# Layer 1's output and MLP products as one 512-column and one 256-column product per k tile, and two adaLN k tiles left to TensorE

## Chip, cores and metric

The kernel runs on one core of one Trainium2 chip. The metric is the device time of one execution in microseconds; it was 1927.91 us as the median of three runs of the kernel before (1926.07 to 1928.13).

## What is computed

A two-layer diffusion trunk over 256 context tokens and 256 latent tokens of width 1024. Only the latent stream of the second layer is returned, so layer 1 needs its output product and its MLP for the 256 latent tokens alone. Cut to what matters here:

```python
sh1, sc1, ga1, sh2, sc2, ga2 = split((c_silu @ mod_w + mod_b), 6)      # adaLN, once for c and once for c_ctx
h = rms_norm(x, norm1_g) * (1 + sc1) + sh1
m = g1 * (y_lru @ w_branch[0]) + g2 * (y_gla @ w_branch[1]) + g3 * (y_att @ w_branch[2])
x = x + ga1 * (m @ w_out)
x = x + ga2 * (square(relu(modulate(x, norm2_g, sh2, sc2) @ mlp_w1)) @ mlp_w2)
```

Products are made to nearly full float32 precision from a rounded high part and a low part of each operand: W·x is taken as Wh·xh + Wh·xl + Wl·xh.

## The kernel before, in words

Activations lie with the channel in the partitions (8 k tiles of 128) and the 512 tokens (context first, then latent) along the free dimension. Every weight is a 128x1024 tile, that is 8 k tiles by 128 output channels. `weight` (L191 to L202) loads it on the SP queue (L194), ScalarE rounds it to the high part `wh` (L200) and VectorE subtracts to get the low part `wl` (L201); three pairs of `wh`, `wl` are kept. `gemm` (L252 to L263) makes one PSUM tile from a weight: for each k tile three matmuls, Wh·xh, Wh·xl and Wl·xh, 512 columns wide in layer 0 and 256 wide where only one half of the tokens is wanted. All matmuls are recorded by the helper `mm` (L212). PSUM has four tiles for these products.

The order around the change in each layer: the branches' `merge` products, where layer 0 has three of branch 1 and eight of branch 2 after the letter "u" of `QORD` (L30, and the loop from L905 on); the output product `out` (8 weights; in layer 0 done first for the context half and then for the latent half, from L938 on); `norm_stats` and `norm_apply` for the second norm after each half (L369 and L399); then the MLP in chunks: `up` (L961 to L967) with 32 weights `w1`, `down` (L969) with 32 weights `w2`. In layer 0 the first five `up` products of the first chunk are also done half by half. In layer 1 all of these are 256 columns wide. `residual` (L930 to L934) adds a product times a per-channel factor into x: one VectorE instruction per 256 columns (L933). `up` takes relu on ScalarE out of PSUM (L965), squares on VectorE out of PSUM (L966) and splits the result (`split_to`, L282 on ScalarE and L283 on VectorE). In layer 1 the high and the low part of an activation lie side by side in one tile: `ytiles` (L472) gives two views of one tile `yp`, with the high part in one 256-column half and the low part in the other. The normed activation has two tiles, `hh` and `hl` (L397).

The adaLN vectors of layer 0 that are not needed at the start (units 2 to 5 of `mod_w`) come from the generator `mods` (L310 to L350), spawned at "u" (L916). It works in halves of 512 output channels, h1 to h8 here: h1 and h2 are unit 2, the gate `ga1`; h3 to h6 are units 3 and 4, the shift and scale of the second norm; h7 and h8 are unit 5. For one half it loads 8 k tiles of `mod_w` (128x512, L319, into the ten buffers `t2` of the helper `tmp`), and for both token kinds sums them times the conditioning scalar: k tile 0 on ScalarE (L339), the other seven on VectorE (L341), so 14 VectorE instructions for a half. Then `mod_cols` (L288) sums over partitions on TensorE with the constant `pick` (8 matmuls, which the trace shows as 16), copies (L296), transposes, and adds the bias (L308). The generator is paced by a model clock that counts matmul columns: each yield (3.0 after each k tile, 2.0 before `mod_cols`) puts its next step that much later among the products. `need` forces the steps that are still missing: L924 asks for unit 2 before the output product, L953 for units 3 and 4 before the second norm's `norm_apply`. The order on an engine is then set by the scheduler of the framework, by priorities and buffers; `norm_stats` and `norm_apply` of the second norm carry a raised priority (L948 and L954).

Of the kernel before, what the change touches and what calls it, by code (L numbers as in the profile page):

```python
# [15 lines left out]
F32 = mybir.dt.float32  # L16
F32R = mybir.dt.float32r
# [6 lines left out]
KT = 8  # L24
# [13 lines left out]
GZP, G0P = 2, 6  # L38
AHEAD = 800
L_SM, L_PT = 4.0, 1.5  # L40
M_A, M_K, M_S = 300, 3.0, 2.0
NDVE = (0, 2, 5)
NL = 2
O_LX, O_LY, O_GQ, O_GK, O_GV, O_GR, O_GZ = 0, 1024, 2048, 2560, 3072, 4096, 5120
# [60 lines left out]
def trunk_kernel(ctx: ExitStack, tc: tile.TileContext, out: bass.AP, d: dict):  # L105
# [17 lines left out]
    def tmp():  # L123
        return t2.tile([128, 512], F32, name="t2")
# [54 lines left out]
    def load_x():  # L179
        x = bigp.tile([128, KT, T], F32, name="big")  # L180
        for k in range(0, KT, 2):
            nc.sync.dma_start(x[:, k:k + 2, :], d["xt"][:, k:k + 2, :])
        return x
# [42 lines left out]
    def tick():  # L226
        while not busy[0] and tasks:
            t = min(tasks, key=lambda t: t[0])
            if t[0] > clock[0]:
                break  # L230
            step(t)

    def spawn(gen):
        tasks.append([clock[0], gen])
# [17 lines left out]
    def gemm(w, xh, xl, c0, c1=T):  # L252
# [9 lines left out]
            mm(ps[:, :n], wl[:, k, :], a, start=False, stop=k == KT - 1)  # L262
        return ps[:, :n]  # L263

    def gemm_tok(l, c, hh, hl, ts):


        ps = {t: ps_mm.tile([128, 512], F32, name="mm") for t in ts}
        for j in range(4):
            wh, wl = (a.rearrange("p (k m) -> p k m", k=2) for a in weight(l, "tok", c, j))  # L270
            for t in ts:
                s = slice(128 * t, 128 * t + 128)
                for i in range(2):
                    k = 2 * j + i
                    tick()
                    mm(ps[t], hh[:, k, s], wh[:, i, :], start=k == 0, stop=False)
                    mm(ps[t], hh[:, k, s], wl[:, i, :], start=False, stop=False)
                    mm(ps[t], hl[:, k, s], wh[:, i, :], start=False, stop=k == KT - 1)
        return ps
# [27 lines left out]
            bia = pc(l, "modb", o, q * m).rearrange("p (j i) -> p j i", j=q).unsqueeze(3).to_broadcast([128, q, m, 2])  # L307
            V.tensor_tensor(dst, src[:, q * h:q * h + q], bia, op=ALU.add)  # L308

    def mods(l, us, pace):  # L310

        halves = [(u, j) for u in us for j in range(2)]

        def load(u, j, k):
            with tc.high_priority(M_A):
                t = tmp()
                nc.sync.dma_start(t, d["mod_w"][l, u][:, k, 512 * j:512 * j + 512])  # L319
            return t  # L320

        def turn():
            if last:
                for _ in last[0]:
                    pass
                if last[2]:
                    done.add((l, last[1]))

        last = None
        for u, j in halves:  # L330
            bs = (0, 1) if l == 0 or u < 2 else (1,)
            acc = [tmp() for _ in bs]
            nx = load(u, j, 0)
            for k in range(KT):
                t, nx = nx, load(u, j, k + 1) if k + 1 < KT else None
                for a, b in zip(acc, bs):
                    c = cs[:, k, b:b + 1]
                    if k == 0:
                        S.activation(a, t, AF.Copy, scale=c)  # L339
                    else:  # L340
                        V.scalar_tensor_tensor(a, t, c, a, op0=ALU.mult, op1=ALU.add)  # L341
                yield pace
            yield M_S
            g = mod_cols(l, 128, lambda i, acc=acc, bs=bs: (pick[:, bs[i], :], lambda c: acc[i][:, c:c + 128]),
                         len(bs), (4 * u if j == 0 else 8 + 4 * u,) if u < 2 else (8 * u + 4 * j,))
            next(g)
            turn()
            last = g, u, j
        yield pace
        turn()  # L350
# [42 lines left out]
    def norm_mul(l, which):  # L393

        a = sm.tile([128, 8, 2], F32, name="amul")
        g = pc(l, "n1" if which == 1 else "n2").unsqueeze(2).to_broadcast([128, 8, 2])
        return (hp.tile([128, KT, T], F32R, name="hh"), hp.tile([128, KT, T], F32R, name="hl"), a, g)  # L397

    def norm_apply(l, which, x, c0, c1, st, hn, ks):  # L399
        n = c1 - c0  # L400
        sh0, sc0 = (0, 8) if which == 1 else (24, 32)
        hh, hl, a, g = hn
        k0, k1, s0, s1 = ks[0], ks[-1] + 1, c0 // 256, c1 // 256
        V.scalar_tensor_tensor(a[:, k0:k1, s0:s1], modT[l][:, sc0 + k0:sc0 + k1, s0:s1], 1.0, g[:, k0:k1, s0:s1],
                               op0=ALU.add, op1=ALU.mult)
        for k in ks:
            h = tmp()
            if k % 2:
                G.tensor_tensor(h[:, :n], x[:, k, c0:c1], st[1][:, :n], op=ALU.mult)
            else:  # L410
                V.tensor_tensor(h[:, :n], x[:, k, c0:c1], st[0][:, :n], op=ALU.mult)
            for s in range(s0, s1):
                c = slice(256 * s - c0, 256 * s - c0 + 256)
                sc, sh = a[:, k, s:s + 1], modT[l][:, sh0 + k, s:s + 1]
                if k in NDVE:
                    V.tensor_scalar(h[:, c], h[:, c], sc, sh, op0=ALU.mult, op1=ALU.add)
                else:
                    S.activation(h[:, c], h[:, c], AF.Identity, scale=sc, bias=sh)
            split_to(hh[:, k, c0:c1], hl[:, k, c0:c1], h[:, :n])
# [41 lines left out]
    for l in range(NL):  # L461
# [443 lines left out]
        for st_ in QORD[l]:  # L905
            if st_ == "q":
                qs[len(qs)] = gqa_q(len(qs))
            elif st_ in "01":
                for g in ((0, 1), (2, 3)):
                    spawn(attend(int(st_), g, *qs[int(st_)]))  # L910
            elif st_ == "f":
                finish()
            elif st_ == "m":
                merge(1, next(mi), y2h, y2l)
            elif st_ == "u" and l == 0:
                spawn(mods(0, range(2, 6), M_K))  # L916
        if l:
            finish()
        mh, ml = ytiles("yh")
# [6 lines left out]
        V.tensor_scalar(ga, modT[l][:, 16:24, :], 0.5, None, op0=ALU.mult)  # L926
        if l == 0:
            x = load_x()

        def residual(i, ps, s0, a, b):  # L930
            for s in range(a // 256, b // 256):
                c = slice(256 * s, 256 * s + 256)
                V.scalar_tensor_tensor(x[:, i, c], ps[:, 256 * s - a:256 * s - a + 256], s0[:, i, s:s + 1], x[:, i, c],  # L933
                                       op0=ALU.mult, op1=ALU.add)  # L934
# [5 lines left out]
            mq = [mod_load(l, 5, h, ("yh", "yl")[h]) for h in range(2)]  # L940
        for a, b in halves:
            for i in range(8):
                residual(i, gemm(weight(l, "out", i), mh, ml, a, b), ga, a, b)
            if hn is None:
                hn = norm_mul(l, 2)
            if last:
                mod_half(l, 5, 0, mq[0])
            with tc.high_priority(NHP):  # L948
                st = norm_stats(x, a, b)
            if last:  # L950
                mod_half(l, 5, 1, mq[1])
                done.add((l, 5))
            need(l, 3, 4)  # L953
            with tc.high_priority(NHP):  # L954
                norm_apply(l, 2, x, a, b, st, hn, range(8))
# [4 lines left out]

        def up(c, i, a, b):  # L961
            uh, ul = hid[c]
            ps = gemm(weight(l, "w1", 8 * c + i), hh, hl, a, b)
            r, r2 = gtmp()[:, :b - a], gtmp()[:, :b - a]
            S.activation(r, ps, AF.Relu)  # L965
            V.scalar_tensor_tensor(r2, ps, 0.0, r, op0=ALU.max, op1=ALU.mult)  # L966
            split_to(uh[:, i, a:b], ul[:, i, a:b], r2)  # L967

        def down(c, i, a, b):  # L969
            residual(i, gemm(weight(l, "w2", c, i), *hid[c], a, b), modT[l][:, 40:48, :], a, b)  # L970

        for c in range(5):
            if c < 4:
                hid[c] = ytiles(("yh", "yl")[c % 2])
                n = NSPL if c == 0 and not last else 0
                for a, b in halves:
                    for i in range(n):
                        up(c, i, a, b)
                for i in range(n, 8):
                    up(c, i, c0, T)  # L980
            if c == 0:
                need(l, 5)
            if c == 4 and not last:
                need(1, 0, 1)
                hn1 = norm_mul(l + 1, 1)
                for a, b in halves[::-1]:
                    for i in range(8):
                        down(3, i, a, b)
                    with tc.high_priority(NHP):
                        norm_apply(l + 1, 1, x, a, b, norm_stats(x, a, b), hn1, range(8))  # L990
            elif c > 0:
                for i in range(8):
                    down(c - 1, i, c0, T)
                    if c == 4:
                        nc.sync.dma_start(out[:, i, :], x[:, i, 256:])
            if l == 0 and c == 0:
                spawn(mods(1, range(5), 1.5 * M_K))
        x1 = x


# [101 lines left out]
```

## Time and profile before

| | |
|---|---|
| median of three runs | 1927.91 us |
| the profiled execution, its own time | 1926.13 us |
| its span, first to last instruction | 1924.3 us |
| TensorE matmul busy | 1819.8 us (95%), 10696 instructions |
| VectorE busy | 1273.0 us (66%), 2137 instructions |
| ScalarE busy | 926.4 us (48%) |
| granted TensorE clock, mean | 0.98 |

Times in the rows are microseconds from the start of the span, unless marked ns. PE is TensorE's matmul side, PEld its weight loads, DVE VectorE, ACT ScalarE, POOL GpSimd, SP the queue that issues DMAs. A matmul's row is longer than the distance to the next one, because matmuls are pipelined; rates are therefore read from the distance between starts. A granted clock of 1.00 is 2.4 GHz, 0.50 is 1.2 GHz. "x16" merges that many instructions into one line, and the bracket at a line's end is the idle time before it and what ended it.

### The profile page before, as it was taken

The page shows a single profiled execution, that of the slowest core. Times are in us where ns is not written, and L with a number is a line of the kernel's source. Part 1 is how long each engine was busy: PE and PEld are TensorE (multiplying, and loading weights), DVE is VectorE, ACT ScalarE, POOL GpSimd, SP SyncE. Part 2 cuts the span into 40 slices and gives each one's busy share as a digit, 9 for nine tenths or more (in the row PEclk, how much of TensorE's full clock was granted, in tenths as well). Part 3 has the DMA queues.
Part 4 walks back from the last instruction along what each step waited for, and adds up shares of the span by engine and source line. Part 5 has one row for each costly group of instructions (what it writes and reads, how often), then busy time and mean ns, then how long its engine had stood idle before and what let it go on. Part 6 is the DMA issues. An engine that isn't in the chain of part 4 may idle for free.

```text
span 1924.3 us, 27716 instructions
## 1 busy us (share of the span) xinstructions
PE 1819.8 (95%) x10696; PEld 1544.4 (80%) x10696; DVE 1273.0 (66%) x2137; ACT 926.4 (48%) x1586; POOL 58.0 (3%) x88
## 2 busy tenths in 40 slices
PE   5998999999999999779999999996999999999999
PEld 4765778887777888778888889764888878999999
DVE  5677764445566984889854448787765677566665
ACT  3778544343443333454332325877654554445442
POOL 1000000000000000010000000000000000000000
PEclk9999999999999999879999999998999999999999
DMA  9322223222221653847643236531433333664654
GB/s 313 99 74 69 68 71 97 76 90 77 66 66 45 224 170 124 271 130 235 209 133 99 93 94 191 159 124 62 129 120 114 123 115 98 240 182 148 186 180 150
DMA packets 91619, 255.66 MB, mean 133 GB/s; under 512 B 9184, under 2 KB 20576, under 8 KB 91488
## 3 DMA queue, kind: packets, MB, share of 16 engines
q1 hardware_dynamic: 91488, 253.90, 41.6%
q8 instruction: 84, 1.38, 0.3%
q14 instruction: 47, 0.39, 0.1%
HBM read 252.82 MB, written 1.05 MB: 132 GB/s over the span
## 4 chain that ended last, share of the span: by engine, by line
PE 58%; issue 30%; DVE 6%; ACT 4%; POOL 1%; DMA 1%; SPq 0%; POOLq 0%; DVEq 0%; ACTq 0%
PE mm L212 49%; PE mx L212 2%; PE mx L744 1%; PE mx L725 1%; DVE wl L201 1%; ACT wh L200 1%; DVE t L341 1%; PE mx L216 1%; PE mx L699 1%; PE mx L510 1%; DMA t<-mod_w 1%; DVE lru L530 0%; PE mx L701 0%; DVE lru L529 0%; ACT lru L614 0%
## 5 line engine op out<-in xcount | busy, mean ns | idle before, releaser
L201 DVE TENSOR_TENSOR wl<-wraw,wh 128x1024 fp32r<-128x1024 f32 x365 | 445.9, 1224 | 297.7 <-ACT wh L200 294.5
L200 ACT CAST wh<-wraw 128x1024 fp32r<-128x1024 f32 x363 | 380.1, 1049 | 539.5 <-PE mm L212 464.2
L212 PE MATMUL mm<-hh,wh 128*128 128x512 f32 (+1 forms) x1448 | 500.3, 346 | 12.7 <-DVE big L933 6.1
L212 PE MATMUL mm<-hl,wh 128*128 128x512 f32 (+1 forms) x1448 | 496.4, 343 | 0.0
L212 PE MATMUL mm<-hh,wl 128*128 128x512 f32 (+1 forms) x1448 | 495.6, 342 | 0.0
L212 PEld LDWEIGHTS mm<-hh,wh 128*128 128x128 f32 x1448 | 276.3, 191 | 46.4 <-issue 9.6
L212 PEld LDWEIGHTS mm<-hl,wh 128*128 128x128 f32 x1448 | 276.0, 191 | 32.6 <-issue 3.5
L212 PEld LDWEIGHTS mm<-hh,wl 128*128 128x128 f32 x1448 | 275.8, 191 | 31.7 <-issue 1.4
L212 PE MATMUL mm<-yh,wh 128*128 128x512 f32 (+1 forms) x640 | 225.2, 352 | 3.3 <-DVE big L933 3.3
L212 PE MATMUL mm<-yh,wl 128*128 128x512 f32 (+1 forms) x640 | 225.0, 352 | 0.0
L212 PE MATMUL mm<-yl,wh 128*128 128x512 f32 (+1 forms) x640 | 223.3, 349 | 0.0
L212 PE MATMUL mm<-yp,wh 128*128 128x256 f32 x1024 | 190.6, 287 | 3.8 <-ACT g L771 2.3
L212 PEld LDWEIGHTS mm<-yp,wh 128*128 128x128 f32 x1024 | 161.1, 193 | 6.0 <-ACT g L771 2.5
L341 DVE SCALAR_TENSOR_TENSOR t<-t,cs,t 128x512 f32<-128x512 f32 x210 | 149.3, 752 | 12.7 <-DMA t<-mod_w 9.0
L212 PE MATMUL mm<-yp,wl 128*128 128x256 f32 x512 | 146.4, 286 | 0.8 <-DVE wl L201 0.8
L212 PEld LDWEIGHTS mm<-yh,wh 128*128 128x128 f32 x640 | 122.4, 191 | 18.7 <-DVE big L933 3.6
L212 PEld LDWEIGHTS mm<-yh,wl 128*128 128x128 f32 x640 | 122.1, 191 | 15.2 <-issue 0.5
L212 PEld LDWEIGHTS mm<-yl,wh 128*128 128x128 f32 x640 | 122.1, 191 | 14.9 <-issue 0.5
L212 PE MATMUL mm<-wh,hh 128*128 128x512 f32 x288 | 115.6, 401 | 18.5 <-ACT t L637 18.1
L212 PE MATMUL mm<-wl,hh 128*128 128x512 f32 x288 | 115.1, 400 | 2.3 <-DVE wl L201 2.3
L212 PE MATMUL mm<-wh,hl 128*128 128x512 f32 x288 | 114.4, 398 | 0.0
L933 DVE SCALAR_TENSOR_TENSOR big<-mm,modT,big 128x256 f32<-128x256 f32 x96 | 44.1, 481 | 89.0 <-PE mm L212 88.9
(223 smaller groups left out, 2223.9 us busy)
## 6 DMA issues: line engine op xcount, KB each, us to landing
wraw<-wt SPq DMA_DIRECT2D x365, 512.0 KB, 3.6
t<-mod_w SPq DMA_DIRECT2D x144, 256.0 KB, 3.9
modw<-mod_w SPq DMA_DIRECT2D x6, 2048.0 KB, 14.3
big<-xt SPq DMA_DIRECT2D x8, 512.0 KB, 5.2
gw<-lruw SPq DMA_DIRECT2D x16, 256.0 KB, 3.5
out<-big SPq DMA_DIRECT2D x8, 128.0 KB, 1.9
t<-glaw SPq DMA_DIRECT2D x8, 96.0 KB, 3.1
t<-ropeg SPq DMA_DIRECT2D x2, 256.0 KB, 2.7
```

The lines of the kernel that those rows point to most:

```text
L200: S.copy(wh, r)
L201: (G if lo == "G" else V).tensor_tensor(wl, r, wh.bitcast(F32), op=ALU.subtract)
L212: P.matmul(o, a, b, **kw)
L216: P.transpose(o, a, ident)
L341: V.scalar_tensor_tensor(a, t, c, a, op0=ALU.mult, op1=ALU.add)
L510: P.matmul(pg, gw[:, 2 * dd + q, :], xc, start=True, stop=True)
L699: P.matmul(psc[:, c], en[:, c], em[:, c], start=True, stop=True)
L725: P.matmul(pu[:, :256], kt[:, 128 * t:128 * t + 128], v_[t], start=True, stop=True)
L744: P.matmul(po[:, :256], a, b, start=j == 0, stop=j == len(mm) - 1)
L933: V.scalar_tensor_tensor(x[:, i, c], ps[:, 256 * s - a:256 * s - a + 256], s0[:, i, s:s + 1], x[:, i, c], op0=ALU.mult, op1=ALU.add)
```

## The change

In layer 1, `out`, `w1` and `w2` go through a new function `gemm_pair`: per k tile one 512-column matmul of the weight's high part with both activation parts, and one 256-column matmul of its low part with the high activation part, added to the first half of the PSUM tile. The two halves are added behind: for `out` and `w2` by two VectorE instructions in place of one (`residual_pair`), for `w1` by a ScalarE copy of the second half and a VectorE add. `hh` and `hl` become two views of one tile `h`. In `mods` for layer 0, units 2 to 5, the last two of the eight k tiles are not summed on VectorE: they are kept and multiplied on TensorE by `cs`, so a half has 10 VectorE instructions in place of 14 and 16 matmuls in place of 8; it yields six times 2.8 in place of eight times 3.0. The pace of layer 1's `mods` stays 4.5.

```diff
+    def gemm_pair(w, xx, high):
+        wh, wl = (a.rearrange("p (k m) -> p k m", k=8) for a in w)
+        ps = ps_mm.tile([128, 512], F32, name="mm")
+        for k in range(KT):
+            tick()
+            mm(ps, wh[:, k, :], xx(k), start=k == 0, stop=False)
+            mm(ps[:, :256], wl[:, k, :], xx(k)[:, high, :], start=False, stop=k == KT - 1)
+        return ps
...
-    def mods(l, us, pace):
+    def mods(l, us, pace, nd=KT):
...
             acc = [tmp() for _ in bs]
+            terms = [(pick[:, b, :], a) for a, b in zip(acc, bs)]
             nx = load(u, j, 0)
             for k in range(KT):
                 t, nx = nx, load(u, j, k + 1) if k + 1 < KT else None
+                if k >= nd:
+                    terms.append((cs[:, k, :], t))
+                    continue
...
-            g = mod_cols(l, 128, lambda i, acc=acc, bs=bs: (pick[:, bs[i], :], lambda c: acc[i][:, c:c + 128]),
-                         len(bs), (4 * u if j == 0 else 8 + 4 * u,) if u < 2 else (8 * u + 4 * j,))
+            g = mod_cols(l, 128, lambda i, terms=terms: (terms[i][0], lambda c: terms[i][1][:, c:c + 128]),
+                         len(terms), (4 * u if j == 0 else 8 + 4 * u,) if u < 2 else (8 * u + 4 * j,))
...
-        return (hp.tile([128, KT, T], F32R, name="hh"), hp.tile([128, KT, T], F32R, name="hl"), a, g)
+        h = hp.tile([128, KT, 2, T], F32R, name="h")
+        return (h[:, :, 0, :], h[:, :, 1, :], a, g, h)
...
-                spawn(mods(0, range(2, 6), M_K))
+                spawn(mods(0, range(2, 6), 2.8, KT - 2))
...
+        def residual_pair(i, ps, s0):
+            for p in (ps[:, :256], ps[:, 256:]):
+                V.scalar_tensor_tensor(x[:, i, 256:], p, s0[:, i, 1:2], x[:, i, 256:], op0=ALU.mult, op1=ALU.add)
+
+        def pair(t):
+            return lambda k: t.t[:, k, :].rearrange("p (a b) -> p a b", a=2)
...
-                residual(i, gemm(weight(l, "out", i), mh, ml, a, b), ga, a, b)
+                if last:
+                    residual_pair(i, gemm_pair(weight(l, "out", i), pair(mh), 1), ga)
+                else:
+                    residual(i, gemm(weight(l, "out", i), mh, ml, a, b), ga, a, b)
...
+            if last:
+                ps = gemm_pair(weight(l, "w1", 8 * c + i), lambda k: hn[4][:, k, :, 256:], 0)
+                S.copy(r, ps[:, 256:])
+                V.tensor_tensor(r, ps[:, :256], r, op=ALU.add)
+                V.scalar_tensor_tensor(r2, r, 0.0, r, op0=ALU.max, op1=ALU.mult)
...
+            if last:
+                residual_pair(i, gemm_pair(weight(l, "w2", c, i), pair(hid[c][0]), 1), modT[l][:, 40:48, :])
...
-                spawn(mods(1, range(5), 1.5 * M_K))
+                spawn(mods(1, range(5), 4.5))
```

## Rows read from the trace of the kernel before

**Rows 1.** The page: busy time by engine, and the 40 slices of PE.

```profile
PE 1819.8 (95%) x10696; PEld 1544.4 (80%) x10696; DVE 1273.0 (66%) x2137; ACT 926.4 (48%) x1586; POOL 58.0 (3%) x88
...
PE   5998999999999999779999999996999999999999
```

**Rows 2.** By stage: length; PE, PEld, DVE, ACT, POOL busy (instructions); clock, DMA share, GB/s.

```profile
635.00:709.00 74.00, 74.00 (x354) 60.51 (x353) 71.78 (x101) 26.11 (x36) 0.00 (x0) 1.00 0.68 220
709.00:784.00 75.00, 75.00 (x458) 65.62 (x457) 38.29 (x53) 26.75 (x38) 0.00 (x0) 1.00 0.44 143
784.00:845.00 61.00, 37.67 (x310) 34.74 (x308) 53.61 (x93) 24.82 (x44) 4.69 (x5) 0.81 0.65 214
845.00:870.00 25.00, 25.00 (x192) 24.14 (x192) 21.68 (x46) 17.57 (x38) 3.60 (x5) 0.86 0.46 145
...
1876.00:1920.00 44.00, 44.00 (x369) 44.00 (x368) 25.30 (x32) 14.36 (x16) 0.00 (x0) 1.00 0.51 162
```

**Rows 3.** Stretches of rows 2, line L341 alone: length; DVE busy (instructions); clock, DMA share, GB/s.

```profile
635.00:709.00 74.00, 48.29 (x70) 1.00 0.68 220
...
784.00:845.00 61.00, 29.60 (x42) 0.81 0.65 214
845.00:870.00 25.00, 2.66 (x4) 0.86 0.46 145
```

**Rows 4.** Timeline of PE: sums with `pick`, and the matmuls after idle time.

```profile
723.33 0.65 PE L212 MATMUL mx<-t,pick 128*32 128x128 f32 x16
...
752.08 0.64 PE L212 MATMUL mx<-t,pick 128*32 128x128 f32 x16
...
806.47 0.43 PE L212 MATMUL mx<-t,pick 128*32 128x128 f32 x8 [2.12 <-DVE t L341]
...
808.18 0.65 PE L212 MATMUL mx<-t,pick 128*32 128x128 f32 x8 [1.02 <-DVE t L341]
819.41 1.23 PE L212 MATMUL mx<-t,pick 128*32 128x128 f32 x16 [10.57 <-DVE t L341]
...
824.30 0.58 PE L212 MATMUL mm<-yh,wh 128*128 128x256 f32 x1 [3.27 <-DVE big L933]
824.68 0.41 PE L212 MATMUL mm<-yl,wh 128*128 128x256 f32 x1
824.90 0.41 PE L212 MATMUL mm<-yh,wl 128*128 128x256 f32 x1
...
843.92 0.55 PE L212 MATMUL mm<-hh,wh 128*128 128x256 f32 x1 [6.08 <-DVE big L933]
```

**Rows 5.** Timeline of the SP queue, then one line of POOL's: the loads around a pause.

```profile
701.55 0.33 SPq L319 DMA_DIRECT2D t<-mod_w  x1
706.00 54.98 SPq L194 DMA_DIRECT2D wraw<-wt  x11
...
784.43 0.43 SPq L319 DMA_DIRECT2D t<-mod_w  x1
...
817.99 0.73 POOL L409 TENSOR_TENSOR t<-big,t 128x256 f32<-128x256 f32 x1 [31.92 <-DVE t L341]
```

**Rows 6.** Chain of waits in order of time: start, length, what; 512 columns, then 256.

```profile
871.97 56.21 PE mm L212 x248
...
1736.35 1.63 PE mm L212 x12
...
1738.09 182.88 PE mm L212 x1524
```

**Rows 7.** Timeline of DVE in layer 1: the last `out`, one `up`, one `down`.

```profile
1727.41 0.48 DVE L933 SCALAR_TENSOR_TENSOR big<-mm,ga,big 128x256 f32<-128x256 f32 x1 [0.31 <-PE mm L212]
...
1822.64 0.42 DVE L966 SCALAR_TENSOR_TENSOR g<-mm,g 128x256 f32<-128x256 f32 x1
1824.04 1.23 DVE L201 TENSOR_TENSOR wl<-wraw,wh 128x1024 fp32r<-128x1024 f32 x1 [0.98 <-ACT wh L200]
...
1895.08 0.48 DVE L933 SCALAR_TENSOR_TENSOR big<-mm,modT,big 128x256 f32<-128x256 f32 x1 [0.70 <-PE mm L212]
```

More of the change, by code (lines that the diff above doesn't have):

```diff
@@ L40 @@
 L_SM, L_PT = 4.0, 1.5
-M_A, M_K, M_S = 300, 3.0, 2.0
+M_A, M_S = 300, 2.0
 NDVE = (0, 2, 5)
@@ L401, in norm_apply @@
         sh0, sc0 = (0, 8) if which == 1 else (24, 32)
-        hh, hl, a, g = hn
+        hh, hl, a, g = hn[:4]
         k0, k1, s0, s1 = ks[0], ks[-1] + 1, c0 // 256, c1 // 256
@@ L962, in up @@
             uh, ul = hid[c]
-            ps = gemm(weight(l, "w1", 8 * c + i), hh, hl, a, b)
             r, r2 = gtmp()[:, :b - a], gtmp()[:, :b - a]
-            S.activation(r, ps, AF.Relu)
-            V.scalar_tensor_tensor(r2, ps, 0.0, r, op0=ALU.max, op1=ALU.mult)
+            if last:
[3 more added lines that the diff above has]
+                V.scalar_tensor_tensor(r2, r, 0.0, r, op0=ALU.max, op1=ALU.mult)
+            else:
+                ps = gemm(weight(l, "w1", 8 * c + i), hh, hl, a, b)
+                S.activation(r, ps, AF.Relu)
+                V.scalar_tensor_tensor(r2, ps, 0.0, r, op0=ALU.max, op1=ALU.mult)
             split_to(uh[:, i, a:b], ul[:, i, a:b], r2)
         def down(c, i, a, b):
-            residual(i, gemm(weight(l, "w2", c, i), *hid[c], a, b), modT[l][:, 40:48, :], a, b)
+            if last:
+                residual_pair(i, gemm_pair(weight(l, "w2", c, i), pair(hid[c][0]), 1), modT[l][:, 40:48, :])
+            else:
+                residual(i, gemm(weight(l, "w2", c, i), *hid[c], a, b), modT[l][:, 40:48, :], a, b)
         for c in range(5):
```

## The prediction

> **What bounds the kernel now.** I read the page first: TensorE's matmul side is busy 95% of the span, and in 40 slices it falls off in the middle, at the sevens of slices 17 and 18 [rows 1]. So TensorE sets the time nearly everywhere, and the question is what a matmul costs where it is full and what it waits for where it is not.
>
> Where it is full, the chain of waits gives rates. In layer 0's MLP, 248 matmuls of 512 columns take 56.21 us, 0.2267 each; in layer 1's MLP, 1524 of 256 columns take 182.88 us, 0.1200 each [rows 6]. The second 256 columns cost 0.1067, so 0.0133 us of every matmul does not depend on its columns.
>
> Where it is not full, the views by stage and the timeline of PE tell the rest. From 784 to 870 us run the second half of layer 0's output product and the MLP products that are done by halves. VectorE is nearly full there, 53.61 of 61 us and then 21.68 of 25, 32.3 us of it the adaLN sums of line L341 [rows 2, 3]. TensorE stands idle 2.12, 1.02 and 10.57 us for those sums, 3.27 and 6.08 us for the residual (L933) behind them in VectorE's order, 23.1 us in all, and comes back at the lower clock: starts of 256 columns are 0.22 apart at 824.68 [rows 4], 1.2 GHz for 2.4. Before that stage VectorE is half idle: from 709 to 784 us it is busy 38.29 of 75, while the SP queue issues no adaLN load between 701.55 and 784.43 [rows 2, 5]. The seventy L341 of halves h1 to h5 lie before 709, 42 of h6 to h8 after 784 [rows 3]. The program explains the pause: the sums with `pick` come 28.75 us apart [rows 4], so the model clock would start h6 at about 781, as the output product's first half ends; the step is left to `need`, which asks for it behind the norm's own buffers, and `norm_apply` then waits 31.92 us on L341 [rows 5].
>
> **Part 1: the paired products.** 8 + 32 + 32 = 72 weights in layer 1, 8 k steps each, 576 steps. Before: 3 x 0.1200 = 0.3600. After: 0.2267 + 0.1200 = 0.3467. The gain is 576 x 0.0133 = 7.7 us, all on the path, since TensorE is busy 44.00 of 44 us there [rows 2, 6]. No row has a 512-column matmul that takes its columns from two places, nor 512 and 256 in turn. Lower end: two places cost like two matmuls, gain 0. Upper end: the extra 0.0133 belongs to loading weights and vanishes with a third of the loads; then 768 columns at 0.2267/512 take 0.3400, gain 11.5. I take the rates as they stand, 7.7, since both widths show the same 0.0133.
>
> The rule that speaks against this part is in the Trainium skill, TensorE: Matmul & The Clock Gate, section on the back-to-back issue gap: a warm matmul takes its columns at 2.4 GHz plus about 2.5 ns. By it joining two would give 576 x 2.5 ns = 1.4 us in place of 7.7, about 1908 for the whole. The rows show 13.3 ns, and they decide.
>
> What is added lies on the other engines. `down` and `out` have a second VectorE instruction of 0.48 us; VectorE idles 0.70 us ahead of each residual in `down` alone. `up` has one more on 256 columns, 0.42 us, in 0.98 us of idle time before the next weight [rows 7]; ScalarE's relu becomes a copy of the same shape. A weight lasts 8 x 0.3467 = 2.77 us for 2.88, so these fit with some 0.1 to 0.4 us spare, and VectorE is busy 25.30 of 44 us in `down` [rows 2]. If that cover were gone, the next weight's low part (L201) would be late, and then its Wl matmul. Twice nothing covers the second residual: before the second norm, when the last output product has come (TensorE's next product waits until 1736.35 [rows 6, 7]), and after the last `down`. I add 2 x 0.4 = 0.8; ends 0 and 2.
>
> The one tile `h` is read and written in the same pieces as the two before it: 0, covered by the norm's own chain; at worst, if writers waited for the whole tile, about one matmul, 0.2.
>
> **Part 2: adaLN of layer 0.** Added on TensorE: 8 more matmuls per half, 16 in the trace, 0.64 us a time [rows 4], 8 halves: +5.1 us, on the path, as they stand among full product stretches. Removed on VectorE: 4 of 14 L341 per half, 32 in all, 0.705 us each in the run after 784 [rows 3]: 22.6 us. SP issues the same loads, in the same order, only sooner.
>
> Moved is the pace. A half yields 6 x 2.8 + 2 = 18.8 for 26, and its own matmuls move the clock more, so I scale the 28.75 us to about 21. From a first sum at 752.08 - 3 x 28.75 = 665.8, about 7 us earlier for the shorter first half, the seventh `pick` comes at 659 + 6 x 21 = 785, where `need` asks for it. So nothing is left to force: h6 and h7 are loaded and summed in the idle VectorE time of 709 to 784, 20 x 0.705 = 14.1 us into 36.7, and `norm_apply` no longer waits for them. Only h8 stays after 784.
>
> The stall itself: the stage holds 192 + 192 + 240 - 214 = 410 products of 256 columns (214 are out by 784), 49.2 us at full clock. Other matmuls there, three sums at 0.64 and two norms', I estimate at 8. TensorE is busy 62.7 of 86 us [rows 2], so some 5.5 us go to the lower clock, and 28.8 are lost with the idle time. After: VectorE has 75.3 - 32.3 = 43.0 us of other work there [rows 2, 3] plus h8's 7.1, 50 in 57, which still leaves waits in an order that is fixed. I let 6 us of 28.8 remain: gain 22.8. Lower end of the gain: only the shorter sums count, below under the first rival. Upper end: 28.8. The buffers speak for keeping some: a waiting half now holds four of ten `t2` tiles (two sums, two raw k tiles) in place of two, so VectorE runs less far ahead.
>
> **The sum**, against the profiled execution's 1926.13 (span 1924.3 and 1.8 around it; it is 1.8 below the median): 1926.1 - 7.7 + 0.8 + 5.1 - 22.8 = **1901.5**. I give 1902.
>
> **The rivals.** *The loads still pause.* If the norm's buffers, and not the pace, hold the loads back from 709 on, three halves are again summed after 784: 30 x 0.705 = 21.2 us for 29.6, and the stall shrinks by 8.4 alone: 1926.1 - 7.7 + 0.8 + 5.1 - 8.4 = 1916. For it: `norm_apply`'s wait on L341 [rows 5] shows that the two share buffers. Against it: h2 to h5, which the clock reached before the norm, ran ahead without trouble. If the stall does not shrink at all, it is 1924.
>
> *The pair does not pay.* If columns from two places cost like two matmuls, part 1 gives nothing and the whole is 1909. Nothing in the profile speaks for it.
>
> *The loads set layer 1's pace.* PEld is busy 44.00 of 44 us [rows 2]; then part 1 gives 11.5 and the whole is 1898. Against it: at 512 columns, where loads are rarer, the extra 0.0133 is the same. It goes with the Trainium skill, Perfetto Trace Analysis, section on the most-contended engine, which judges TensorE by the busy share of weight loads and not of matmuls; no row here shows the loads binding.
>
> *Slower: `pick` waits inside the merges.* TensorE works in order. Each half's sum now needs four tiles at once, two fresh from DMA, with less run-ahead; if h2 to h7 each hold TensorE up, the products behind them wait. One such wait took 10.57 us [rows 4]; half of it six times is 31.7, total 1933. It decides from 26/6 = 4.3 us a half. For it: VectorE is 97% busy from 635 to 709 [rows 2]. Against it: 10 sums need 7 us of a 21 us period, and the merges leave VectorE half free.
>
> **How the numbers follow.** Forecast 0.56; the pause stays 0.23, of which 0.06 where it shrinks so little that the time is within 0.2%; the pair does not pay 0.05; the loads set the pace 0.06; slower 0.10. 0.2% is 3.9 us of 1927.9, about what a measurement of this kernel can tell from no change. Faster: 0.56 + 0.17 + 0.05 + 0.06 = 0.84, same 0.06, slower 0.10. The forecast with the whole stall gone and the loads' price is 1892; I go from 1893, and up to 1919 so that the first rival is in but its tail and the slower case are out.
>
> **What the changed profile would show.** 178 L341 for 210; 10248 matmuls (10696 - 576 + 128). In layer 1 the chain of waits as one stretch with 0.3467 us per pair, and starts 0.227 and 0.120 apart; 0.360 would be the second rival. AdaLN loads on SP through 709 to 784, at most ten or so L341 after it, `pick` rows about 21 us apart, no idle bracket over 3 us at them, clock 1.00 from 784 to 870. Wrong would be: thirty or more L341 still after 784, `pick` rows with idle time ahead of them in the merges, or in layer 1 matmuls that wait on `wl`.

## The result, and the profile after

The changed kernel takes **1900.42 us** (median of four runs, 1897.52 to 1903.26) for 1927.7 of the kernel before on the same chip: a ratio of **0.986, 95% interval 0.9838 to 0.9882**, faster by 27 us. The forecast was 1902 in 1893 to 1919. The profiled execution took 1897.52 us, span 1895.7.

The page of the kernel after, for the rows of [rows 1] and the adaLN sums:

```profile
PE 1810.9 (96%) x10248; PEld 1509.6 (80%) x10248; DVE 1282.9 (68%) x2177; ACT 924.8 (49%) x1586; POOL 57.1 (3%) x88
...
PE   5998999999999999999999999996999999999999
...
L356 DVE SCALAR_TENSOR_TENSOR t<-t,cs,t 128x512 f32<-128x512 f32 x178 | 127.2, 746 | 24.1 <-DMA t<-mod_w 15.1
```

The two sevens of the slices have become nines. The old L341 is now L356, 178 times for 210. The same stretches as in [rows 2], after:

```profile
635.00:709.00 74.00, 74.00 (x410) 60.40 (x409) 55.85 (x78) 24.67 (x35) 0.00 (x0) 1.00 0.67 210
709.00:784.00 75.00, 74.97 (x521) 64.76 (x519) 54.35 (x78) 30.23 (x44) 0.00 (x0) 1.00 0.66 212
784.00:845.00 61.00, 57.08 (x491) 54.97 (x483) 52.80 (x100) 37.08 (x73) 7.46 (x10) 1.00 0.62 203
845.00:870.00 25.00, 25.00 (x124) 21.16 (x123) 24.88 (x40) 12.86 (x21) 0.00 (x0) 1.00 0.75 235
```

Three things to see, each against [rows 2]: from 784 to 845 TensorE is busy 57.08 us for 37.67; its clock is 1.00 throughout, for 0.81 and 0.86; and VectorE works 54.35 us between 709 and 784, where it worked 38.29. The adaLN sums alone, for [rows 3]:

```profile
709.00:784.00 75.00, 20.39 (x29) 1.00 0.66 212
784.00:845.00 61.00, 8.67 (x12) 1.00 0.62 203
```

Before, none of them began between 709 and 784, and 42 stood between 784 and 845. The work has moved from the crowded stretch into the empty one. Timeline of PE after, a sum with `pick` among the merges and every wait from 806 to 834:

```profile
700.06 0.65 PE L212 MATMUL mx<-t,pick 128*32 128x128 f32 x16
700.52 0.62 PE L212 MATMUL mx<-t,cs 128*32 128x128 f32 x16
701.08 0.33 PE L216 MATMUL mx<-ident,t 128*128 128x128 f32 x1
...
808.17 0.36 PE L212 MATMUL mm<-yh,wh 128*128 128x256 f32 x1 [2.36 <-DVE big L957]
820.61 0.68 PE L403 MATMUL mx<-t,ones 128*128 128x128 f32 x4 [0.50 <-DVE t L402]
832.98 0.50 PE L212 MATMUL mm<-h,wh 128*128 128x256 f32 x2 [0.78 <-DVE g L999]
```

3.64 us of idle time are left of the 23.1 in [rows 4]. Timeline of SP after, the last adaLN loads around the gap that was 701.55 to 784.43 in [rows 5]:

```profile
763.80 0.35 SPq L330 DMA_DIRECT2D t<-mod_w  x1
796.33 1.67 SPq L330 DMA_DIRECT2D t<-mod_w  x3
```

A pause of 32.5 us is left, for 82.9 before; seven of the eight halves are loaded ahead of it, where five were.

And the end of the chain of waits in layer 1, for the last line of [rows 6]:

```profile
1715.56 176.30 PE mm L212 x1017
```

176.30 us for 508.5 pairs are 0.3467 us each, where 182.88 for 508 were 0.3600.

**Where the time went.** I cut the run at two instructions that both kernels have: A, the last transposes of layer 0's keys, and B, the first matmul of layer 1's output product. Timelines of PE, first the kernel before, then after:

```profile
480.20 0.40 PE L835 MATMUL mx<-ident,t 128*128 128x128 f32 x2
...
1703.86 0.40 PE L212 MATMUL mm<-yp,wh 128*128 128x256 f32 x2
```

```profile
479.89 0.41 PE L851 MATMUL mx<-ident,t 128*128 128x128 f32 x2
...
1681.41 0.40 PE L212 MATMUL mm<-yp,wh 128*128 128x512 f32 x1
```

A to B holds all of layer 0's adaLN change: 1223.66 before, 1201.52 after, **22.1 us less**. B to the end of the span holds the pairs: 1924.3 - 1703.86 = 220.4 before, 1895.7 - 1681.41 = 214.3 after, **6.1 less**. The start up to A gives 0.3. In sum 28.6, the difference of the two spans.

### The profile page after: what moved, and what is told of

Read it like the earlier page. It is cut to its first block, busy times and chain, and to the rows that moved or that the text cites. A ratio compares the mean times of both kernels' runs of the same rounds, so it can differ in the third digit from the quotient of the medians.

```text
span 1895.7 us, 26828 instructions
## 1 busy us (share of the span) xinstructions
PE 1810.9 (96%) x10248; PEld 1509.6 (80%) x10248; DVE 1282.9 (68%) x2177; ACT 924.8 (49%) x1586; POOL 57.1 (3%) x88
## 4 chain that ended last, share of the span: by engine, by line
issue 49%; PE 39%; DVE 5%; ACT 4%; POOL 2%; DMA 0%; SPq 0%; POOLq 0%; ACTq 0%; DVEq 0%
PE mm L212 31%; PE mx L212 2%; PE mx L760 1%; PE mx L741 1%; DVE wl L201 1%; ACT wh L200 1%; PE mx L715 1%; PE mx L526 1%; POOL t L425 1%; PE mx L216 1%; DVE lru L546 0%; PE mx L717 0%; DVE lru L545 0%; ACT lru L630 0%; ACT lru L527 0%
## 5 line engine op out<-in xcount | busy, mean ns | idle before, releaser
L212 PE MATMUL mm<-h,wh 128*128 128x512 f32 (+1 forms) x2640 | 733.3, 360 | 8.3 <-DVE wh L198 4.5
L212 PEld LDWEIGHTS mm<-h,wh 128*128 128x128 f32 x2640 | 468.3, 189 | 85.4 <-issue 6.6
L212 PE MATMUL mm<-h,wl 128*128 128x512 f32 (+1 forms) x1448 | 493.2, 341 | 0.0
L212 PEld LDWEIGHTS mm<-h,wl 128*128 128x128 f32 x1448 | 273.8, 189 | 31.9 <-issue 1.4
L212 PE MATMUL mm<-wh,h 128*128 128x512 f32 x576 | 187.3, 400 | 18.5 <-ACT t L653 18.1
L212 PE MATMUL mm<-yp,wh 128*128 128x256 f32 (+1 forms) x704 | 186.0, 338 | 3.8 <-ACT g L787 2.3
L356 DVE SCALAR_TENSOR_TENSOR t<-t,cs,t 128x512 f32<-128x512 f32 x178 | 127.2, 746 | 24.1 <-DMA t<-mod_w 15.1
L212 PEld LDWEIGHTS mm<-wh,h 128*128 128x128 f32 x576 | 109.7, 191 | 42.3 <-ACT t L653 18.9
L212 PE MATMUL mm<-wl,h 128*128 128x512 f32 x288 | 115.2, 400 | 2.0 <-DVE wl L201 2.0
L212 PEld LDWEIGHTS mm<-yp,wl 128*128 128x128 f32 x512 | 97.1, 190 | 1.0 <-issue 1.0
L212 PE MATMUL mx<-t,t 128*128 128x128 f32 (+2 forms) x416 | 81.8, 338 | 0.0
L957 DVE SCALAR_TENSOR_TENSOR big<-mm,modT,big 128x256 f32<-128x256 f32 x64 | 28.6, 480 | 66.8 <-PE mm L212 66.8
```

Of the source, the lines that this page charges most:

```text
L212: P.matmul(o, a, b, **kw)
```

## The experiments

All runs in one table. "A to B" as above, from each one's profile; "DVE" and "GB/s" are VectorE's busy time and the DMA rate from 709 to 784 us; "last stretch" is the last line of the chain of waits, layer 1's MLP. Each ratio is against runs of the kernel before on the same chip, taken beside it. Runs taken beside each other are e1 to e4, then e5, e7 and e9, then e6 and e8, then e10 to e12; from group to group the kernel before has medians of 1925.56 to 1927.7, so that medians of two groups do not tell 2 us apart. A to B repeats better: the changed kernel's two profiles, after and e9, have 1201.52 and 1201.49.

| kernel | median us | ratio, 95% interval | A to B | DVE | GB/s | last stretch |
|---|---|---|---|---|---|---|
| before | 1927.7 | | 1223.7 | 38.3 | 143 | 182.88 |
| after | 1900.42 | 0.986, 0.9838 to 0.9882 | 1201.5 | 54.4 | 212 | 176.30 |
| e1 pairs only | 1922.42 | 0.998, 0.9971 to 0.999 | 1222.6 | 38.3 | 145 | 179.59 |
| e2 adaLN only | 1906.33 | 0.9902, 0.9888 to 0.9917 | 1202.3 | 54.5 | 211 | 182.88 |
| e3 quicker pace, no raw tiles | 1907.99 | 0.9909, 0.9891 to 0.9927 | 1208.4 | 50.0 | 178 | 176.30 |
| e4 raw tiles, halves as far apart as before | 1914.33 | 0.9941, 0.9924 to 0.9959 | 1214.4 | 45.2 | 176 | 176.27 |
| e5 high product in two | 1905.3 | 0.9889, 0.9874 to 0.9903 | 1202.3 | | | 182.89 |
| e6 asked for first | 1895.14 | 0.984, 0.982 to 0.9859 | 1194.7 | 63.7 | 218 | 179.59 |
| e7 pairs in the merges too | 1899.29 | 0.9858, 0.9843 to 0.9873 | 1200.9 | | | 179.59 |
| e8 four raw tiles | 1900.51 | 0.9867, 0.9848 to 0.9887 | 1202.4 | 46.6 | 222 | 176.30 |
| e9 after, again | 1902.55 | 0.9876, 0.986 to 0.9893 | 1201.5 | | | 179.59 |
| e10 after, asked for first | 1894.49 | 0.9834, 0.982 to 0.9847 | 1198.2 | 56.7 | 218 | 176.27 |
| e11 e6 and e7 | 1892.24 | 0.9823, 0.981 to 0.9837 | 1192.7 | 63.6 | 218 | 179.59 |
| e12 two units asked for first | 1909.44 | 0.991, 0.9897 to 0.9924 | 1211.3 | 47.5 | 167 | 179.60 |

### The two parts alone (e1, e2)

e1 is the changed kernel with the adaLN of before:

```diff
-                spawn(mods(0, range(2, 6), 2.8, KT - 2))
+                spawn(mods(0, range(2, 6), 3.0))
```

> The changed kernel with adaLN of layer 0 as before (all eight k tiles summed on VectorE, pace 3.0); the paired products and the one tile h stay. Theory (0.0133 us of each matmul does not depend on its columns): the last matmul of layer 1 less the first of its output product shrinks by 6.5 to 7.5 us against the kernel before, layer 0 is unchanged, the whole is 1919 to 1921. If the pair did not pay: 1926 to 1928. If the loads set the pace: 1915.

e2 is the other way round, `gemm_pair` gone from `out`, `up` and `down`:

```diff
-                if last:
-                    residual_pair(i, gemm_pair(weight(l, "out", i), pair(mh), 1), ga)
-                else:
-                    residual(i, gemm(weight(l, "out", i), mh, ml, a, b), ga, a, b)
+                residual(i, gemm(weight(l, "out", i), mh, ml, a, b), ga, a, b)
...
```

> The changed kernel with the products of layer 1 as before (three 256-column matmuls per k step); adaLN as changed. Theory (the two parts are separate and add): 1897.5 + 6.7 = 1904 in the quicker of the two levels that the changed kernel showed, 1910 in the other; the stage from 784 us looks as in the changed kernel. If the parts depended on each other, the sum of this run's gain and that of the run with the pairs alone would miss 28 us by more than 3.

The pairs alone give 3.7 us against the 1926.15 of the kernel before beside them, the adaLN part 19.8. e1's 1922.42 lies above the 1919 to 1921 that its theory gave, e2's 1906.33 within its 1904 to 1910. In e1 the stage stands as it was; its timeline of PE has the old brackets:

```profile
808.08 0.42 PE L212 MATMUL mx<-t,pick 128*32 128x128 f32 x8 [2.78 <-DVE t L356]
809.78 0.66 PE L212 MATMUL mx<-t,pick 128*32 128x128 f32 x8 [1.02 <-DVE t L356]
820.59 1.23 PE L212 MATMUL mx<-t,pick 128*32 128x128 f32 x16 [10.15 <-DVE t L356]
825.50 0.58 PE L212 MATMUL mm<-yh,wh 128*128 128x256 f32 x1 [3.27 <-DVE big L957]
845.26 0.77 PE L212 MATMUL mm<-h,wh 128*128 128x256 f32 x2 [6.08 <-DVE big L957]
```

The two gains add up to 23.5 us, 4.5 short of 28, and a miss of more than 3 was to be the sign that the parts depend on each other. The stretches put the shortfall elsewhere. From A to B, e1 takes off 1.0 and e2 21.4, 22.4 together for the changed kernel's 22.1: there the parts add. From B to the end e1 takes off 3.2 and e2 adds 0.9, where the changed kernel's first profile takes off 6.1 and its second (e9) 3.5. The rest lies ahead of A, where neither part has begun. So the shortfall is for the most part in the pairs, which brought half of the 7.7 us that they were priced at, and not always the same in one and the same kernel. Why is the matter of e5 and e9, below.

### Which half of the adaLN part: pace or raw tiles (e3, e4)

e3 keeps all k tiles on VectorE and takes a quicker pace, a half yielding 18.8 as in the changed kernel (8 x 2.1 + 2); e4 keeps the two raw tiles and yields 26 as before (6 x 4.0 + 2).

```diff
-                spawn(mods(0, range(2, 6), 2.8, KT - 2))
+                spawn(mods(0, range(2, 6), 2.1))
```

```diff
-                spawn(mods(0, range(2, 6), 2.8, KT - 2))
+                spawn(mods(0, range(2, 6), 4.0, KT - 2))
```

> The changed kernel with all eight k tiles summed on VectorE again, but paced 8 x 2.1 + 2 = 18.8 for a half, as the changed kernel's halves. Theory A (the pace does it: the halves are asked for before the second norm): no pause of the loads from 701 to 784, the stall at 804 to 844 stays small, and without the raw tiles' 16 extra matmul rows a half the whole is 1893 to 1900. Theory B (the fewer VectorE sums do it): the stall comes back in the most part, 1912 to 1922.

> The changed kernel with the raw tiles, but paced 6 x 4.0 + 2 = 26 for a half, as the halves before. Theory A (the pace does it): the loads pause again ahead of 784, about 30 of L341's kind stand after it, and only the shorter sums help: 1908 to 1916. Theory B (the fewer VectorE sums do it): as the changed kernel, 1897 to 1904.

e3's 1907.99 us lies between its two theories, e4's 1914.33 where theory A had it. From e1's A to B of 1222.6, e3 takes off 14.2, e4 8.2, the changed kernel 21.1. But e3 is not the changed kernel's pace alone. Two of its sums in the timeline of PE:

```profile
706.40 0.65 PE L212 MATMUL mx<-t,pick 128*32 128x128 f32 x16
729.71 0.64 PE L212 MATMUL mx<-t,pick 128*32 128x128 f32 x16
```

They are 23.3 us apart, for 21.0 in the changed kernel: `tick` takes a step only at the next k step of a product, and e3 has eight steps to round up where the changed kernel has six. Six of its sums are out by 784, for seven. So e3 shows what a pace between the two gives; how much of the change is pace and how much raw tiles, these two runs do not divide. Each leaves a pause of the loads (e3 from 729.74, e4 from 753.21, both to 786 or 788), and each a stall. The waits of TensorE, 640 to 900, in e3 and then e4 (us in total, times, longest):

```profile
PE mm L212 <- DVE big L957: 10.2, 1, 10.2
...
PE mx L212 <- DVE t L356: 0.2, 1, 0.2
```

```profile
PE mm L212 <- DVE big L957: 5.8, 1, 5.8
PE mx L212 <- DVE t L356: 3.2, 3, 1.4
PE mm L212 <- ACT h L293: 2.8, 1, 2.8
```

In the table, from e1 by e4 and e3 to the changed kernel, A to B falls as VectorE's work between 709 and 784 rises, whatever brought the work there (e8, below, has fewer sums to bring and stands outside this row). That pointed away from "less work" and towards "work in time".

### When the columns are asked for (e6, e12, e10)

e6 takes e1, whose adaLN is that of before in pace and in work, and moves one request: units 3 and 4 are asked for ahead of the output product and not behind the second norm's statistics.

```diff
-                spawn(mods(0, range(2, 6), 2.8, KT - 2))
+                spawn(mods(0, range(2, 6), 3.0))
...
-        need(l, 2)
+        need(l, 2, 3, 4)
```

> The kernel with the pairs and the adaLN of before (pace 3.0, no raw tiles; e1), with one edit: all of the adaLN of units 2 to 4 is asked for ahead of layer 0's output product, where before units 3 and 4 are asked for behind it. Theory A (the wait arises because the last halves are still spread out when their columns are asked for, so that DVE's chains for them land inside the output product's end; where they are issued earlier the time closes): the long bracket of 10 us and the two of 3 to 6 us go, the first pick of layer 0's second stage comes at 915 to 918 for 932.7 and the time is near 1907. Theory B (the vector engine's work and the loads that wait for its buffers set it, not where the columns are asked for): the same wait only stands elsewhere, ahead of the output product's first residuals, the loads still pause, and the time stays at 1918 to 1925.

It takes 1895.14 us: 27.3 below e1, and 5.3 below the changed kernel by the medians (the two intervals overlap), with the old pace and all 210 sums on VectorE. Windows of e6, for [rows 2]:

```profile
635.00:709.00 74.00, 74.00 (x354) 60.54 (x353) 71.51 (x101) 26.53 (x37) 0.00 (x0) 1.00 0.68 227
709.00:784.00 75.00, 75.00 (x491) 64.70 (x490) 63.74 (x98) 29.88 (x45) 0.00 (x0) 1.00 0.68 218
784.00:845.00 61.00, 59.37 (x480) 57.14 (x480) 52.25 (x97) 40.14 (x77) 7.24 (x10) 1.00 0.63 202
```

Where the sums went shows in two timelines of DVE around 745 us, first the kernel before, then e6:

```profile
747.65 1.22 DVE L201 TENSOR_TENSOR wl<-wraw,wh 128x1024 fp32r<-128x1024 f32 x1 [4.21 <-ACT wh L200]
```

```profile
744.50 1.22 DVE L201 TENSOR_TENSOR wl<-wraw,wh 128x1024 fp32r<-128x1024 f32 x1
745.64 2.85 DVE L356 SCALAR_TENSOR_TENSOR t<-t,cs,t 128x512 f32<-128x512 f32 x4
748.40 1.22 DVE L201 TENSOR_TENSOR wl<-wraw,wh 128x1024 fp32r<-128x1024 f32 x1
```

Before, VectorE waits 4.21 us for the next weight's high part, merge after merge; in e6 four sums stand in that gap. All of TensorE's waits from 640 to 900 in e6:

```profile
PE mm L212 <- DVE g L999: 0.6, 1, 0.6
PE mx L403 <- DVE t L402: 0.5, 1, 0.5
PE mx L216 <- ACT t L307: 0.2, 1, 0.2
```

So theory A of e6 holds, and goes further than it expected (1907). Neither VectorE's load nor the buffers were short: the halves were asked for too late in the order of the work.

e12 asks for units 2 and 3 first and leaves unit 4 where it was.

```diff
-        need(l, 2, 3, 4)
+        need(l, 2, 3)
```

> e6 with units 2 and 3 asked for ahead of layer 0's output product and unit 4 behind it, as before: two late halves for none in e6 and four in e1. Theory A (the late vector work is what TensorE waits for: two halves of some 14 chain steps of 0.7 us, 20 us, for four): the stall is well under half of e1's, as the output product's second half and the first products behind it cover part of the 20 us: first pick of layer 0's second stage at 907 to 916, time 1898 to 1907. Theory B (the loads of unit 4, held behind weight loads in SP's queue, set the end whatever number of halves is late): a pause of the loads of 40 us or more and one long bracket remain, that pick at 920 to 933, the time 1911 to 1922.

1909.44 us, between the two expectations: the loads pause from 722.42 to 784.97 and the first `pick` of the second stage comes at 922.81, as theory B has it, but there is no long bracket. TensorE's waits from 640 to 900 are spread:

```profile
PE mm L212 <- ACT h L293: 5.8, 1, 5.8
PE mx L212 <- DVE t L356: 3.6, 2, 1.9
PE mm L212 <- DVE big L957: 2.7, 1, 2.7
PE mm L212 <- DVE g L999: 2.5, 1, 2.5
```

From e1 to e6 A to B falls by 27.9, to e12 by 11.3: fewer late halves cost less, but one late unit still costs more than half of the whole stall. That fits the norm, which needs its scale as well as its shift, so that the last to come decides; it was not tried apart.

e10 puts e6's request into the changed kernel.

```diff
-        need(l, 2)
+        need(l, 2, 3, 4)
```

> The changed kernel (pairs, two raw tiles, pace 2.8) with the adaLN of units 2 to 4 asked for ahead of layer 0's output product, as in e6. Theory A (where the columns are asked for is the cause, and raw tiles and pace only lighten the late load): nothing is left for raw tiles to win, and they still cost their column matmuls, about 0.5 us in each of eight halves, so about 4 us above e6: the first pick of layer 0's second stage at 907 to 909 (e6 904.1), the time 1897 to 1900. Theory B (the two remedies add): that pick before 903 and a time under 1893.

A to B is 1198.2, 3.5 above e6: with the request moved, raw tiles and pace win nothing and cost their column matmuls, as theory A had it (about 4). In time theory A missed: the median of 1894.49 is no worse than e6's, against 1897 to 1900. e10's profile has the quicker of two pair rates (176.27 us in the last stretch) and e6's the slower (179.59), which is 3.3 us. Whether e10 or e6 is the quicker is not settled by these runs.

### Twice the raw tiles (e8)

```diff
-                spawn(mods(0, range(2, 6), 2.8, KT - 2))
+                spawn(mods(0, range(2, 6), 4.2, KT - 4))
```

> The changed kernel with one edit: four raw k tiles in each half of layer 0's spread-out adaLN for two, at a pace (4.2 for 2.8) that keeps the halves as far apart in TensorE's work: twice the raw tiles. Theory A (a raw tile costs its column matmuls alone): 32 more single-column matmuls in each of eight halves, about 0.5 us by what pick and columns take in the changed kernel (32 in about 1.0 us), so 3 to 5 us more, 1901 to 1908, with picks still about 21 us apart and no bracket over 3 us ended by them. Theory B (the rival of the prediction, raw tiles hold their buffers until the pick, so the next loads come late and TensorE waits at the pick in the merges): bursts of six loads behind a pick, idle of 1 us or more at most picks, some 8 us or more on top, 1910 or above.

Theory A in kind, with no wait at a `pick`; in size it is 1900.51 us, below theory A's 1901 to 1908. (A half has 16 more matmuls in the trace's count, not the 32 of the expectation, and the halves come closer: the `pick` rows are 18.8 us apart for the changed kernel's 21.0.) Timeline of PE, one half, to set beside that of the changed kernel above:

```profile
695.15 0.65 PE L212 MATMUL mx<-t,pick 128*32 128x128 f32 x16
695.62 1.06 PE L212 MATMUL mx<-t,cs 128*32 128x128 f32 x32
696.60 0.33 PE L216 MATMUL mx<-ident,t 128*128 128x128 f32 x1
```

From `pick` to the transposes it is 1.45 us for 1.02: 0.43 for 16 more, 3.4 in eight halves. TensorE's waits up to 900 are 1.3 us for 3.7, and so A to B grows by 0.9 alone. The buffers held until the `pick` cost nothing here.

### What a pair costs (e5, e9)

e5 gives the 512-column matmul as two of 256, with all else of the pair kept.

```diff
-            mm(ps, wh[:, k, :], xx(k), start=k == 0, stop=False)
+            mm(ps[:, :256], wh[:, k, :], xx(k)[:, 0, :], start=k == 0, stop=False)
+            mm(ps[:, 256:], wh[:, k, :], xx(k)[:, 1, :], start=False, stop=False)
```

> The changed kernel with one edit: in layer 1's pair products the 512-column matmul is given as two of 256 columns into the same accumulator, with everything behind it (two residuals, ACT copy and DVE sum) kept. Theory A (the gain of part 1 is the joining of two matmuls into one of 512 columns): every k step goes back from 0.3475 or 0.3542 us to 3 x 0.1200 = 0.3600, 576 steps give 7.2 us (from the quicker rate) or 3.3 (from the slower), so about 1904.7 us, layer 1 from the first output product to the last product at 217.1 to 218 us, and the executions lie close together, as in the kernel before (no two levels 5.7 us apart). Theory B (the order of the weights, each high part's two matmuls back to back, is what pays, whatever their width): the second of two matmuls on the same weights starts sooner than 0.120 us behind the first, and the time stays at 1897.5 to 1903.

Theory A: 1905.3 us, runs within 1.7 us of each other, and the last stretch back at the 182.88 of before. So it is the joining that pays; whether what it saves is a matmul's or that of the weight load that goes with each, no run divides. (Theory B's order of the weights could not be what paid: `gemm` in the kernel before has each high part's two matmuls back to back too.) e9 is the changed kernel once more.

> The changed kernel as it is, once more. Theory A (a pair's rate is fixed for an execution, at one of two values, 0.3475 or 0.3542 us): single times gather near 1897.5 and 1903.3, nothing much between, and the profile of this run shows one of the two rates in every chunk of 64 pairs, 0.3475 with a time near 1897.5, 0.3542 near 1903.3. Theory B (the spread comes from elsewhere, say from waits on loads in layer 0): times spread evenly, or the profile's rate does not go with its time.

The last line of the chain of waits in e5 and then in e9, for the 176.30 of the changed kernel's first profile:

```profile
1716.28 182.89 PE mm L212 x1524
```

```profile
1716.17 179.59 PE mm L212 x1017
```

**A pair has two rates**: 176.30/508.5 = 0.3467 and 179.59/508.5 = 0.3532. (The expectations of e5, e7 and e9 call them 0.3475 and 0.3542, which is 0.001 too high.) In the eleven profiles with pairs, the output product's stretch and the MLP's each go at 0.3466 to 0.3468 or at 0.3531 to 0.3536, with nothing between. The same program shows both (after and e9), and one execution can show both: in the changed kernel's first profile the output product's unbroken run of starts goes at 0.3536 and the MLP's at 0.3467, in e9 at 0.3468 and 0.3533. So e9's theory A is wrong in that the rate belongs to an execution: it belongs to a stretch without a wait, and keeps to its end. Layer 1's MLP in 256 columns alone (before, e2, e5) always took 0.1200 a matmul, and layer 0's MLP in 512 alone, read from starts over 167 and more in a row, took 0.2268 to 0.2270 in the changed kernel and in every experiment. Rows of one stretch, the changed kernel's first profile and then e9, starts of 512 and 256 columns in turn:

```profile
1790.46 0.39 PE L212 MATMUL mm<-h,wh 128*128 128x512 f32 x1
1790.69 0.27 PE L212 MATMUL mm<-h,wl 128*128 128x256 f32 x1
1790.80 0.40 PE L212 MATMUL mm<-h,wh 128*128 128x512 f32 x1
```

```profile
1790.64 0.40 PE L212 MATMUL mm<-h,wh 128*128 128x512 f32 x1
1790.88 0.28 PE L212 MATMUL mm<-h,wl 128*128 128x256 f32 x1
1791.00 0.40 PE L212 MATMUL mm<-h,wh 128*128 128x512 f32 x1
```

All 576 pairs at the slower rate cost 576 x 0.0065 = 3.7 us more. What sets the rate is open; nothing was tried on it. e9's single times (1901.38, 1901.42, 1903.68, 1904.08) do not show the expected pair of values 5.7 us apart either; A itself comes between 478.8 and 482.6 us from profile to profile, so single times hold more than the rate.

### Pairs in the merges, and all together (e7, e11)

In layer 1's `merge` both products become pairs, each summed by a ScalarE copy and a VectorE add.

```diff
-            pb = gemm(weight(l, "br", b, i), yh, yl, c0)
+                pb = gemm_pair(weight(l, "br", b, i),
+                               lambda k: yh.t[:, k, :].rearrange("p (a b) -> p a b", a=2), 1)
...
+                S.copy(v, pb[:, 256:])
+                V.tensor_tensor(v, pb[:, :256], v, op=ALU.add)
```

> The changed kernel with the pair products in layer 1's 24 merges too: 48 products of eight k steps, 384 pairs, each followed by an ACT copy and a DVE sum. Theory A (a pair is worth 0.3600 less its measured 0.3475 or 0.3542, wherever TensorE has no wait): 384 x 0.0125 = 4.8 us less at the quicker rate, 384 x 0.0058 = 2.2 at the slower; as the sums stand beside matmuls the time is 1893 (all executions at the quicker rate) to 1901, median near 1896. Theory B (in the merges the longer drain, copy, sum, Tanh, holds an accumulator back and TensorE waits for it): at some 0.5 us for each of 24 merges the gain is gone and more, 1905 or above, with idle TensorE time ended by the copies or sums.

1899.29 us, within theory A's 1893 to 1901 and 3.3 below e9, taken beside it, though the two intervals overlap. The merges' pairs ran at both rates, 85 in a row at 0.3533 and 64 in a row at 0.3467. And there is a price, perhaps that of the adds in VectorE's order, which was not tried apart: at the score matmuls of line L715 where e9 waits 0.31 us, e7 waits 4.74. Timeline of PE in e7:

```profile
1380.29 0.98 PE L715 MATMUL mx<-t,t 128*128 128x128 f32 x3 [4.74 <-DVE t L710]
```

> e6 (pairs in layer 1's output and MLP products, adaLN at pace 3.0 without raw tiles, units 2 to 4 asked for first) with pairs in layer 1's merges too (e7). Theory A (a merge's two products take 2 x 2.77 or 2 x 2.83 us for 2 x 2.88, and the transposes that waited 4.7 us in e7 for 0.3 to 1.2 in the changed kernel wait so again): 48 x 0.05 to 0.11 = 2.4 to 5.1 us won and 3 to 4 given back, so within 2 us of e6, 1893 to 1896. Theory B (that wait of e7 was an accident of its order): 2.4 to 5 us below e6, 1889 to 1892.

e11 takes **1892.24 us** (1890.09 to 1893.99), the quickest of all runs, 35 us below before and some 8 below the changed kernel. It is 2.9 below e6, one more than theory A allowed, though the two intervals overlap, and A to B is 2.0 shorter than e6's. The wait at L715 stands here too (4.7 us), so theory B's reason is wrong. The merges' pairs seem worth 2 to 3 us net of it, which these runs do not set clear of noise.

## Why the prediction was right, and where it was off

The sum was 24.6 us off the profiled 1926.13, and 28.6 came. That the forecast of 1902 and the median of 1900.42 lie so close is in part luck: the adaLN part gave more than its 17.7 us (22.1 from A to B, 19.8 in e2) and the pairs less than their 6.9 (6.1 from B to the end, 3.7 in e1), and the two misses work against each other. By its steps:

- **The stall, 22.8 of 28.8.** Right in its place, and short by 2.4: it let 6 us of waits remain, and 3.64 remained. With the column matmuls below this makes 4.0 of the 4.4 us by which A to B shrank more than the 17.7 forecast. What it argued from the model clock, that h6 to h8 come late only because the request stands behind the norm, is shown by e6, which changes that request alone and takes A to B down by 27.9. The prediction read the cause and then priced two remedies that lighten it; it did not see that they are not needed.
- **Fewer sums and quicker pace.** 178 L356, `pick` rows 21.0 us apart, the seventh at 783.14 (785 forecast), clock 1.00. Of the at most ten late sums there were six, the last at 810.19. The 31 L356 that stand between 784 and 870 are not the thirty that would have been a sign of being wrong: those from 832.84 on are already layer 1's. The loads ran through the old gap up to 763.80, not to 784.
- **Column matmuls, 5.1.** Mis-sized: 16 more rows take 0.43 us by e8 and 0.45 by e6 (1.02 us from `pick` to the transposes, 0.57 in e6), 3.4 to 3.6 in eight halves. The 3.5 of e10 less e6 agrees. The 0.64 in [rows 4] is the length of a pipelined row, where the way to the next instruction counts.
- **Pairs, 7.7.** Right at the quicker rate, 0.3467 to the digit; half of it at the slower, which no row of before could show. The profiled execution had the quicker one in the 64 MLP weights. Of the two uncovered residuals (0.8) the one at the end took 0.51: the span ends 3.85 us behind the last matmul, for 3.34 before and 3.38 in e2, which has no second residual. The one before the second norm took some 0.2 at most. There are 9.55 us between the two products for 8.91 before, but e2 has 9.46 without the residual, and e4, e7, e11 and e12 have 9.03 to 9.09 with it. What differs is a wait of VectorE for ScalarE in the norm (L427, before L411): 1.52 us after and 1.58 in e2, 1.07 before and in e12. Its cause is open.
- **The rivals.** "The loads still pause" failed as put: the norm's buffers do not hold them (e6: they go on to 760.88). "The pair does not pay" is what e5 looks like, and it is not what the change does. "The loads set layer 1's pace" would give 0.3400, and no stretch shows it, though PEld, busy all of layer 1's MLP before, is busy 152.08 of 174 us after. "`pick` waits inside the merges": no bracket there, not even with four raw tiles (e8).

On the price of a matmul beside its columns: e5 against the changed kernel says (182.89 - 176.30)/508 = 0.0130 us for each join at the quicker rate and 0.0065 at the slower. The Trainium skill, TensorE: Matmul & The Clock Gate, section on the back-to-back issue gap, has a warm matmul at its columns plus about 2.5 ns, which the section calls the gap of an isolated matmul. Both prices here, in a stream with weight loads, lie above that, and the measurement decides.

## What to carry to other kernels

When an engine waits in one stage for work that another engine could have done in its gaps a stage earlier, first look at where the work is asked for in the program's order: moving one request (e6) took 27.9 us off e1's A to B, where making the work smaller and quicker (the change) took off 21.1. Read a price from the distance between starts, not from the length of a row that is pipelined. Two products that share their stationary weight are worth joining wherever TensorE has no other wait, and a term that rests on such a rate wants more than one execution.

## What the hardware showed unexpectedly

Matmuls of 512 and 256 columns in turn, on an engine that never waits and at a granted clock of 1.00, run at 0.3467 or 0.3533 us a pair, fixed over 499 pairs in a row, and changing from stretch to stretch and from execution to execution of one program. 256 columns alone (layer 1's MLP before, in e2 and in e5) and 512 alone (layer 0's MLP) each show one rate, 0.1200 and 0.227.
